# A hybrid decoder block on one core: the attention heads' last transposes and a LayerNorm's reductions go through DRAM instead of TensorE

## The chip, the cores and the metric

One core of a Trainium2 chip runs the whole kernel in one launch. The metric is the time of an execution on the device in microseconds; lower is better. The engines run side by side, each with its own in-order queue: TensorE (PE in the profile, its weight loads PEld), VectorE (DVE), ScalarE (ACT), GpSimd (POOL), and SyncE (SP), which issues nearly all DMAs.

## The reference

One layer over 512 tokens of width 2048, in float32:

```
h = RMSNorm(x);  proj = h @ W_in                       # 30 column tiles of 128
A: 8 heads x 64, dilated causal attention: the mixture of (window, dilation)
   (128,1), (512,4), (2048,16), combined by the softmax denominators
B: 512 channels: u * sigmoid(g) -> causal depthwise conv of 31 taps
   -> LayerNorm over channels -> silu
   mu = mean(y); var = mean((y - mu)^2); y = (y - mu) * rsqrt(var + EPS) * g + b
C: 16 query heads, 2 kv heads x 64, causal window of 128, with sinks
x = x + concat(A, B, C) @ W_out
x = x + (silu(RMSNorm(x) @ W_gate) * (RMSNorm(x) @ W_up)) @ W_down
```

In the A heads the weights exp(s) (queries in the partitions) have to be turned so that the keys stand in the partitions, to be multiplied by the values.

## The kernel before

Each float32 product is made of three matmuls on parts: a high part and a low part of both sides (`wh`, `wl` of the weights; `h_hi`, `h_lo` of the tokens), `wh*xh + wh*xl + wl*xh`, each 128x512. ScalarE casts the high parts (L295), VectorE subtracts to get the low ones (L269), two units of 128x1024 ahead of use, in three buffers each.

The stages are, in order: a head that projects the first four column tiles as the tokens come in; the other 26 projections of 16 x 3 matmuls (`project`), with the three mixers woven in; the output projection, in two halves of 16 tiles with 8 x 3 matmuls each (L1223 and on; the tiles' results are added to x by `residual`, L1166); the gated FFN by Strassen-like products (L1372 to L1375), and its down projection (L1637 to L1639).

What is woven in is set by hand. `Ticks` counts steps; a step passes after every two groups of three matmuls (in the output projection's second half after four). `ticks.after(n, fn)` puts `fn` n steps on, and at that step all engines' queues get the instructions that `fn` writes. So the place of everything relative to TensorE's queue is a number in the source, and a queue that is late keeps what stands behind it. The projections take the steps 0 to 207, the output projection begins at 208 (`T_MEET`), its second half at 272.

An A head (`attention("a", ...)`, one call for two heads) makes its scores in three units (`UNITS["a"]`): query blocks 0 and 1 together, block 2 (three key blocks), block 3 (four). For each: scores, scaling on ScalarE (L941), bias and minimum on VectorE (L946), exponentials on ScalarE (L954). Ten 128x128 blocks of weights result. Eight of them are turned through DRAM:

- `blocks_turn` (step t0+10): VectorE turns 32x32 squares into a 128x1024 tile `z` (L971).
- `blocks_leave` (two steps later): SP writes `z` to DRAM (`ed`, L976).
- `blocks_back` (three later): SP waits for that and reads it back by four strided DMAs into `et` (L983).
- `blocks_high`, `blocks_low` (five and six later): ScalarE's high copies `ph` (L993), VectorE's low parts `pl` (L999).

The other two blocks (key block 2 of query blocks 2 and 3) are turned by TensorE in `flip`: two transposes into a PSUM bank (L1006), with `high` (L1012) and `low` (L1017) behind. `weigh` multiplies all by the values (L1030, L1031). The heads come at least 8 steps apart; a0 and a1 lie in the projections, a2 and a3 in the output projection (t0 = 204, 212, 220 and 228).

In the same queues each q and k tile has a chain of its own for its RMS norm (`head_scales`): VectorE's turning sum, four small DMAs (L659), one back (L664), three POOL operations (L672 to L674); q's result scales the logits (L941).

The convolution is 124 operations of VectorE (`tap`, L590), spread over the steps by `TAP_TICKS`, with a pause round step 208. The LayerNorm behind it starts at `T_LN + 2`: `ln_sum` (L599 to L601), `ln_split` and `ln_center` (the mean through TensorE, `lnm`, L617 and L618), `ln_square`, then `ln_var`, where `transposed_scale` turns the squares' sum by four transposes (L486), reduces them on VectorE (L487) and takes the power on POOL (L489). `ln_out` spreads the scales to all partitions by four more transposes (L480) and multiplies (L633). `split_mix` makes the two parts of each row of the concatenation (L1085, L1086) for the output projection, which takes the `b` rows in its second half.

The RMS norm ahead already has another way for the same: `token_scale` and `spread`, with VectorE's turning sums and small DRAM trips.

Of the kernel before, what the change touches and what calls it, by code (L numbers as in the profile page):

```python
# [10 lines left out]
F32 = mybir.dt.float32  # L11
F32R = mybir.dt.float32r
# [3 lines left out]
ALU = mybir.AluOpType  # L16

P = 128
T = 512
NT = T // P  # L20
# [4 lines left out]
EPS = 1e-6  # L25
# [8 lines left out]
OUT_ORDER = (list(range(16)), [n + o for n in range(6) for o in (0, 8)] + [6, 7, 14, 15])  # L34

TAP_TICKS = (1.4, 1.5, 1.9, 1.9)
T_LN = 244
T_MEET = 208
T_GLU = 14

# [1 line left out]
SD, KD, VD, EV = 11, 6, 13, 1  # L42
# [79 lines left out]
def kernel(ctx: ExitStack, tc: tile.TileContext, xT, wi, wo, wgu, wd, cst_in, outT):  # L122
    nc = tc.nc
# [17 lines left out]
    ticks = Ticks()  # L141

    def slot(name, dt=F32, cols=T):
        return sp.tile([P, cols], dt, name=name, tag="s")

    def bank(name, cols=T, pool="banks"):
        return psum[pool].tile([P, cols], F32, name=name, tag="b")
# [64 lines left out]
    for t, (g, r) in enumerate(DOWN):  # L212
# [7 lines left out]
        for k in ("21A", "11A", "21B", "11B", "22A", "22B", "12A", "12B"):  # L220
            c = k[2]
# [130 lines left out]
    b = bank("idle")  # L352
# [4 lines left out]
    b = idle = None  # L357

    nhalf = cp.tile([P, 8], F32, name="nhalf")
# [3 lines left out]
    ident = cp.tile([P, P], F32, name="ident")  # L363
# [6 lines left out]
    def small(name, cols=NT):  # L370
        return cp.tile([P, cols], F32, name=name, tag="small", bufs=8)
# [56 lines left out]
    def token_scale(acc, n, name, after, then):  # L428

        part = cp.tile([P, NT, NT], F32, name=name + "p", tag="hsp", bufs=3)  # L430
        nc.vector.tensor_reduce(part.rearrange("p l b -> p b l"), acc.rearrange("p (b l c) -> p b l c", b=NT, l=NT),
                                axis=mybir.AxisListType.X, op=ALU.add, apply_transpose=True)

        def leave():
            d = tc.dram_tile([P, NT * NT], F32, name=name + "d")
            for a in range(4):
                nc.sync.dma_start(d.rearrange("(l i) (a b) -> i l a b", i=32, a=4)[:, :, a], part[32 * a:32 * a + 32])
            after(2, back, d)

        def back(d):  # L440
            t = cp.tile([P, 4, NT], F32, name=name + "t", tag="hst", bufs=3)
            nc.sync.dma_start(t.rearrange("p a b -> p (a b)"), d)
            after(3, power, t)

        def power(t):
            v = small(name + "v")
            wide = cp.tile([P, 64], F32, name=name + "w")
            r = wide[:, :NT]
            nc.gpsimd.memset(wide[:, NT:32], 0.0)
            nc.gpsimd.tensor_add(t[:, :2], t[:, :2], t[:, 2:])  # L450
            nc.gpsimd.tensor_add(v, t[:, 0], t[:, 1])
            nc.vector.tensor_scalar(v, v, 1.0 / n, EPS, op0=ALU.mult, op1=ALU.add)
            nc.gpsimd.tensor_tensor(r, v, nhalf[:, :NT], op=ALU.pow)
            then(v, r, wide)

        after(1, leave)
# [17 lines left out]

        ticks.after(2, turn)

    def spread_by_tensor(src4, name):
        b = bank(name)
        for i in range(NT):
            nc.tensor.transpose(b[:, i * P:(i + 1) * P], src4[:, i:i + 1].to_broadcast([P, P]), ident)  # L480
        return b

    def transposed_scale(acc, n, name):
        t, v, r = bank(name), small(name + "v"), small(name + "r")
        for i in range(NT):
            nc.tensor.transpose(t[:, i * P:(i + 1) * P], acc[:, i * P:(i + 1) * P], ident)  # L486
        nc.vector.tensor_reduce(v, t.rearrange("p (a b) -> p a b", b=P), axis=mybir.AxisListType.X, op=ALU.add)  # L487
        nc.vector.tensor_scalar(v, v, 1.0 / n, EPS, op0=ALU.mult, op1=ALU.add)
        nc.gpsimd.tensor_tensor(r, v, nhalf[:, :NT], op=ALU.pow)  # L489
        return r  # L490

    g4 = [bank(f"in{j}") for j in range(HEAD4)]
    h_hl = {}
    late_lows.append(True)
# [8 lines left out]
    for k in range(KT):  # L503
# [9 lines left out]
        elif k < 4 or k % 2 == 0:  # L513
            wh, wl = next_unit()
            o = 0
# [54 lines left out]
    hconv, yconv = {}, {}  # L570
# [24 lines left out]
    ln = {}  # L595
# [29 lines left out]
            add_square(ln["s"], yconv[j], j, "lq")  # L625

    def ln_var():
        ln["r"] = transposed_scale(ln.pop("s"), 512, "lv")

    def ln_out(mix):  # L630
        b = spread_by_tensor(ln["r"], "lrs")
        for j in range(NB):
            nc.vector.tensor_mul(yconv[j], yconv[j], b)  # L633
        for j in range(NB):
            nc.scalar.activation(yconv[j], yconv[j], AF.Silu, bias=col(C_LB + j), scale=col(C_LG + j))
            mix[f"b{j}"] = yconv[j]
# [179 lines left out]
    def attention(kind, box, mix, mi, heads):  # L816
        ready, every, step, s1, sx, s2, fl, ev, we = C_TICKS if kind == "c" else A_TICKS

        if mi in ROWS[-2:]:
            fl, we = fl + 2, we  # L820
        name = mi
# [29 lines left out]
        def head(h):  # L851
# [104 lines left out]

            ph, pl = {}, {}

            def block(i, j):
                for u, un in enumerate(us):  # L960
                    for ii, k0, n, o in un:
                        if ii == i:
                            f = o + j * P - k0
                            return es[u][:, f:f + P]

            def blocks_turn():
                z = wp.tile([P, 1024], F32, name=f"{name}z{h}", tag=f"raw{TURN_BUFS[0]}", bufs=1)
                to = z.rearrange("p (j b q) -> p b j q", j=4, b=8)
                for u, c, bs in ((0, slice(0, 2), slice(0, 2)), (0, slice(2, 3), slice(4, 5)), (1, slice(0, 2), slice(2, 6, 3)),
                                 (2, slice(0, 2), slice(3, 7, 3)), (2, slice(3, 4), slice(7, 8))):  # L970
                    nc.vector.transpose(to[:, bs], es[u].rearrange("p (b j q) -> p b j q", b=NT, j=4)[:, c])  # L971
                ticks.after(2, blocks_leave, z)

            def blocks_leave(z):
                d = tc.dram_tile([P, 1024], F32, name=f"{name}ed{h}")
                nc.sync.dma_start(d, z)  # L976
                ticks.after(3, blocks_back, d)

            def blocks_back(d):
                turned[0] = 3 - turned[0]  # L980
                t = wp.tile([P, 1024], F32, name=f"{name}et{h}", tag=f"raw{TURN_BUFS[turned[0]]}", bufs=1)
                for j in range(4):
                    nc.sync.dma_start(t[32 * j:32 * j + 32].rearrange("p (i c) -> p i c", i=4),  # L983
                                      d.rearrange("(i p) c -> p i c", i=4)[:, :, j * 2 * P:(j + 1) * 2 * P])
                ticks.after(5, blocks_high, t.rearrange("p (i b q) -> p b i q", i=4, b=8))

            def queries4(t):
                return t.rearrange("p (b i q) -> p b i q", b=NT, i=4)

            def blocks_high(src):  # L990
                for t in range(2):
                    ph[t] = slot(f"{name}ph{h}{t}", F32R)
                    nc.scalar.copy(queries4(ph[t]), src[:, NT * t:NT * t + NT])  # L993
                ticks.after(EV, blocks_low, src)

            def blocks_low(src):
                for t in range(2):
                    pl[t] = slot(f"{name}pl{h}{t}", F32R)
                    nc.vector.tensor_sub(queries4(pl[t]), src[:, NT * t:NT * t + NT], queries4(ph[t]).bitcast(F32))  # L999

            def flip(t):
                b = bank(f"{name}t{h}{t}")
                o = 0
                for j, i0, i1 in TBANKS[kind][t]:
                    for i in range(i0, i1 + 1):
                        nc.tensor.transpose(b[:, o:o + P], block(i, j), ident)  # L1006
                        o += P
                ticks.after(ev, high, t, b, o)

            def high(t, b, o):  # L1010
                ph[t] = slot(f"{name}ph{h}{t}", F32R)
                nc.scalar.copy(ph[t][:, :o], b[:, :o])  # L1012
                ticks.after(EV, low, t, b, o)

            def low(t, b, o):
                pl[t] = slot(f"{name}pl{h}{t}", F32R)
                nc.vector.tensor_sub(pl[t][:, :o], b[:, :o], ph[t][:, :o].bitcast(F32))  # L1017

            def weigh():
                b = bank(f"{name}o{h}")  # L1020
# [41 lines left out]
            if kind == "c":  # L1062
                ticks.after(tu, packed_exps)
                ticks.after(tu + s2, packed_norm)
                ticks.after(tu + 1, packed_turn)
            else:
                ticks.after(tu + s2, invert, h, den)
                ticks.after(tu + 2, blocks_turn)
                ticks.after(tu + s2 + fl + 2, flip, 2)
            ticks.after(t0 + at_v, weigh)  # L1070
            if h == 1:
                ticks.after(t0 + at_v - 2, sums_back)
# [21 lines left out]
    t_tap = T_GLU + 2  # L1094
    for j in range(NB):
        for i in range(TAPS):
            if T_MEET - 3 <= t_tap < T_MEET + 7:
                t_tap = T_MEET + 7
            ticks.after(int(t_tap), tap, j, i)
            t_tap += TAP_TICKS[j]  # L1100
    t_ln = T_LN
# [3 lines left out]
    ticks.after(t_ln + 4, ln_center)  # L1105
    ticks.after(t_ln + 6, ln_square)
    ticks.after(t_ln + 11, ln_var)
    ticks.after(t_ln + 14, ln_out, mix)
    for n, row in enumerate(r for r in ROWS if r[0] == "b"):
        ticks.after(t_ln + 15 + n, split_mix, row)  # L1110

    shared = {}
    cooling.append(True)
# [679 lines left out]
```

## Time and profile before

| | |
|---|---|
| Time, median of 3 runs | 1826.38 us (1826.2 to 1826.75) |
| Profiled execution | 1827.03 us, span 1825.3 us, clock 0.999 |
| TensorE busy | 1818.3 us, 8191 matmuls |
| VectorE, ScalarE, GpSimd busy | 1434.5, 1327.6, 1022.1 us |
| Output projection, first half | 375.5 to 474.4 us from the span's start |

A row of a timeline gives the start in us from the span's start, the length, the engine, the line and the operands (out<-in), the count of merged instructions, and in brackets the idle time before it and what ended that. Groups give the busy time, the mean length of one in ns, and the idle time ahead. Lists of waits give total, count and longest. Rows of stretches give for each engine the busy time and the count of instructions, then the granted clock, the DMA engines' busy share and GB/s. Matmuls overlap, so their lengths add up to more than the time that they take of the queue.

### The profile page before, as it was taken

What the parts mean: (1) busy time and instruction counts of PE and PEld (TensorE: products, weight loads), DVE (VectorE), ACT (ScalarE), POOL (GpSimd) and SP (SyncE); (2) the same over time, 40 slices, a digit from 0 to 9 for tenths busy, and PEclk for the clock granted to TensorE, in tenths of its full rate; (3) what the DMA queues carried; (4) which work ended last, traced back from release to release, by engine and by line L of the source; (5) the groups of instructions that cost most, each with busy time, mean ns of one, the idle gap of its engine ahead of it and who ended that gap; (6) DMA issues with size and microseconds to landing.
All of it is one profiled execution on the core that took longest, in us unless ns stands there. A gap on an engine that the chain in (4) does not pass through costs nothing.

```text
span 1825.3 us, 26570 instructions
## 1 busy us (share of the span) xinstructions
PE 1818.3 (100%) x8191; PEld 1509.9 (83%) x8191; DVE 1434.5 (79%) x1996; ACT 1327.6 (73%) x1848; POOL 1022.1 (56%) x793
## 2 busy tenths in 40 slices
PE   9999999999999999999999999999999999999998
PEld 7888888888888888888888888888888888888887
DVE  6779999987689777777777777777777777777777
ACT  6345656664468778888888888888887778877775
POOL 0116555120014577786887868878775568775652
PEclk9999999999999999999999999999999999999999
DMA  7355456666343557787777877778687579877645
GB/s 279 96 161 157 152 172 182 195 211 214 130 145 113 130 142 206 191 222 192 194 205 191 220 192 197 204 190 223 176 278 261 195 230 293 259 256 255 231 127 105
DMA packets 409295, 354.61 MB, mean 194 GB/s; under 512 B 177088, under 2 KB 331840, under 8 KB 409152
## 3 DMA queue, kind: packets, MB, share of 16 engines
q1 hardware_dynamic: 408576, 352.12, 65.7%
q8 instruction: 65, 1.06, 0.2%
q10 hardware_dynamic: 576, 0.79, 0.1%
q14 instruction: 78, 0.64, 0.1%
HBM read 270.00 MB, written 74.41 MB: 189 GB/s over the span
## 4 chain that ended last, share of the span: by engine, by line
PE 99%; DVE 1%; DMA 0%; issue 0%; ACT 0%; SPq 0%; DVEq 0%; ACTq 0%
PE out L1374 15%; PE out L1375 15%; PE out L1372 15%; PE out L1637 7%; PE out L1639 7%; PE out L1638 7%; PE o L328 3%; PE o L330 3%; PE o L329 3%; PE cq L328 2%; PE cq L329 2%; PE cq L330 2%; PE ak L328 1%; PE aq L328 1%; PE av L328 1%; PE ak L330 1%
## 5 line engine op out<-in xcount | busy, mean ns | idle before, releaser
L1372 PE MATMUL out<-wh,h 128*128 128x512 f32 x1232 | 479.2, 389 | 0.0
L1374 PE MATMUL out<-wl,h 128*128 128x512 f32 x1232 | 479.2, 389 | 0.0
L1375 PE MATMUL out<-wh,h 128*128 128x512 f32 x1232 | 479.2, 389 | 0.0
L1372 PEld LDWEIGHTS out<-wh,h 128*128 128x128 f32 x1232 | 231.2, 188 | 48.1
L1374 PEld LDWEIGHTS out<-wl,h 128*128 128x128 f32 x1232 | 231.2, 188 | 48.1
L1375 PEld LDWEIGHTS out<-wh,h 128*128 128x128 f32 x1232 | 231.2, 188 | 47.9
L1637 PE MATMUL out<-wh,a 128*128 128x512 f32 x620 | 240.4, 388 | 0.0
L1638 PE MATMUL out<-wl,a 128*128 128x512 f32 x620 | 240.3, 388 | 0.0
L1639 PE MATMUL out<-wh,a 128*128 128x512 f32 x620 | 240.3, 388 | 0.0
L295 ACT CAST wh<-w 128x1024 fp32r<-128x1024 f32 (+2 forms) x94 | 97.0, 1032 | 115.8 <-PE o L329 48.9
L1647 DVE TENSOR_TENSOR y<-y,out 128x512 f32<-128x512 f32 x192 | 128.6, 684 | 47.6 <-PE out L1639 46.1
L269 DVE TENSOR_TENSOR wl<-w,wh 128x1024 fp32r<-128x1024 f32 (+2 forms) x95 | 114.1, 1203 | 30.0 <-ACT wh L295 28.9
L1639 PEld LDWEIGHTS out<-wh,a 128*128 128x128 f32 x620 | 116.4, 188 | 24.0
L1638 PEld LDWEIGHTS out<-wl,a 128*128 128x128 f32 x620 | 116.4, 188 | 23.8
L1637 PEld LDWEIGHTS out<-wh,a 128*128 128x128 f32 x620 | 116.4, 188 | 23.8
L590 DVE SCALAR_TENSOR_TENSOR y<-bu,cst,y 128x511 f32<-128x511 f32 (+14 forms) x120 | 89.8, 748 | 0.5
L328 PE MATMUL o<-mh_c,wh 128*128 128x512 f32 x128 | 50.3, 393 | 0.0
L328 PE MATMUL cq<-hh,wh 128*128 128x512 f32 x128 | 50.0, 391 | 0.0
L329 PE MATMUL cq<-hl,wh 128*128 128x512 f32 x128 | 49.9, 390 | 0.0
L329 PE MATMUL o<-ml_c,wh 128*128 128x512 f32 x128 | 49.9, 390 | 0.0
L330 PE MATMUL o<-mh_c,wl 128*128 128x512 f32 x128 | 49.9, 390 | 0.0
L330 PE MATMUL cq<-hh,wl 128*128 128x512 f32 x128 | 49.8, 389 | 0.0
(2359 smaller groups left out, 4736.4 us busy)
## 6 DMA issues: line engine op xcount, KB each, us to landing
od<-a SPq DMA_DIRECT2D x154, 256.0 KB
a<-od SPq DMA_DIRECT2D x154, 256.0 KB
w<-in_wi SPq DMA_DIRECT2D x58, 512.0 KB
w<-in_wo SPq DMA_DIRECT2D x32, 512.0 KB
x<-in_xT SPq DMA_DIRECT2D x16, 256.0 KB
xr<-in_xT SPq DMA_DIRECT2D x16, 256.0 KB
x2d<-xr SPq DMA_DIRECT2D x16, 256.0 KB
z<-x2d SPq DMA_DIRECT2D x64, 64.0 KB
```

Of the source, the lines that this page charges most:

```text
L269: fn(*args)
L295: (nc.vector.tensor_copy if u == 0 else nc.scalar.copy)(hi[:, :n], t[:, :n])
L328: nc.tensor.matmul(out, wh, xh, start=start, stop=False)
L329: nc.tensor.matmul(out, wh, xl, start=False, stop=False)
L330: nc.tensor.matmul(out, wl, xh, start=False, stop=stop)
L1372: nc.tensor.matmul(b, x[:, high], wh[:, s], start=c == f == 0 and q in (7, 1, 5, 2), stop=False, skip_group_check=True)
L1374: nc.tensor.matmul(b, x[:, high], wl[:, s], start=False, stop=False, skip_group_check=True)
L1375: nc.tensor.matmul(b, x[:, low], wh[:, s], start=False, stop=c == f == 1, skip_group_check=True)
L1637: nc.tensor.matmul(b[:, lo:hi], x[:, high], wh[:, s], start=start, stop=False, skip_group_check=True)
L1638: nc.tensor.matmul(b[:, lo:hi], x[:, high], wl[:, s], start=False, stop=False, skip_group_check=True)
L1639: nc.tensor.matmul(b[:, lo:hi], x[:, low], wh[:, s], start=False, stop=last, skip_group_check=True)
L1647: getattr(eng, op)(t, t, src)
```

## The change

1. All ten blocks of an A head go through DRAM. `blocks_turn` makes a second tile `z2` (128x256) with two more turns, `blocks_leave` writes it, `blocks_back` reads it back by four DMAs into `t2`, and `blocks_high` and `blocks_low` make three copies and three subtractions instead of two. `block`, `flip`, `high`, `low` go. The exponentials' tiles are let go at `blocks_turn`.
2. The LayerNorm's variance takes `token_scale` and `spread` in place of the eight transposes; `spread_by_tensor` and `transposed_scale` go.
3. `T_LN` goes from 244 to 231, so `ln_sum` comes at step 233 instead of 246. From `ln_var` to `ln_out` there are 15 steps instead of 3, so `ln_out` comes at 259 instead of 260.
4. The pause of the taps ends at step 211 instead of 215.

```diff
-T_LN = 244
+T_LN = 231
...
     def ln_var():
-        ln["r"] = transposed_scale(ln.pop("s"), 512, "lv")
+        ln["r"] = slot("lrs")
+        token_scale(ln.pop("s"), 512, "lv", ticks.after, lambda v, r, wide: spread(wide, "l", ln["r"]))
 
     def ln_out(mix):
-        b = spread_by_tensor(ln["r"], "lrs")
         for j in range(NB):
-            nc.vector.tensor_mul(yconv[j], yconv[j], b)
+            nc.vector.tensor_mul(yconv[j], yconv[j], ln["r"])
...
                     nc.vector.transpose(to[:, bs], es[u].rearrange("p (b j q) -> p b j q", b=NT, j=4)[:, c])
-                ticks.after(2, blocks_leave, z)
+                z2 = slot(f"{name}z{h}", cols=2 * P)
+                to = z2.rearrange("p (j b q) -> p b j q", j=4, b=2)
+                for n in range(2):
+                    nc.vector.transpose(to[:, n], es[n + 1][:, 2 * P:3 * P].rearrange("p (j q) -> p j q", j=4))
+                es.clear()
+                ticks.after(2, blocks_leave, z, z2)
 
-            def blocks_leave(z):
+            def blocks_leave(z, z2):
                 d = tc.dram_tile([P, 1024], F32, name=f"{name}ed{h}")
                 nc.sync.dma_start(d, z)
-                ticks.after(3, blocks_back, d)
+                d2 = tc.dram_tile([P, 2 * P], F32, name=f"{name}ec{h}")
+                nc.sync.dma_start(d2, z2)
+                ticks.after(3, blocks_back, d, d2)
...
+                t2 = slot(f"{name}eu{h}", cols=2 * P)
+                for j in range(4):
+                    nc.sync.dma_start(t2[32 * j:32 * j + 32].rearrange("p (i c) -> p i c", i=4),
+                                      d2.rearrange("(i p) c -> p i c", i=4)[:, :, j * 64:(j + 1) * 64])
...
-            def flip(t):
-                b = bank(f"{name}t{h}{t}")
-                o = 0
-                for j, i0, i1 in TBANKS[kind][t]:
-                    for i in range(i0, i1 + 1):
-                        nc.tensor.transpose(b[:, o:o + P], block(i, j), ident)
-                        o += P
-                ticks.after(ev, high, t, b, o)
...
-                ticks.after(tu + s2 + fl + 2, flip, 2)
...
-            if T_MEET - 3 <= t_tap < T_MEET + 7:
-                t_tap = T_MEET + 7
+            if T_MEET - 3 <= t_tap < T_MEET + 3:
+                t_tap = T_MEET + 3
...
-    ticks.after(t_ln + 14, ln_out, mix)
+    ticks.after(t_ln + 26, ln_out, mix)
     for n, row in enumerate(r for r in ROWS if r[0] == "b"):
-        ticks.after(t_ln + 15 + n, split_mix, row)
+        ticks.after(t_ln + 27 + n, split_mix, row)
```

More of the change, by code (lines that the diff above doesn't have):

```diff
@@ L475, in spread @@
         ticks.after(2, turn)
[L477 to L490, printed above, removed]
     g4 = [bank(f"in{j}") for j in range(HEAD4)]
@@ L957, in head @@
             ph, pl = {}, {}
[L959 to L964, printed above, removed]
             def blocks_turn():
@@ L971, in blocks_turn, with blocks_back @@
                     nc.vector.transpose(to[:, bs], es[u].rearrange("p (b j q) -> p b j q", b=NT, j=4)[:, c])
-                ticks.after(2, blocks_leave, z)
-            def blocks_leave(z):
+                z2 = slot(f"{name}z{h}", cols=2 * P)
[5 more added lines that the diff above has]
+            def blocks_leave(z, z2):
                 d = tc.dram_tile([P, 1024], F32, name=f"{name}ed{h}")
                 nc.sync.dma_start(d, z)
-                ticks.after(3, blocks_back, d)
-            def blocks_back(d):
+                d2 = tc.dram_tile([P, 2 * P], F32, name=f"{name}ec{h}")
+                nc.sync.dma_start(d2, z2)
+                ticks.after(3, blocks_back, d, d2)
+            def blocks_back(d, d2):
                 turned[0] = 3 - turned[0]
@@ L984, in blocks_back @@
                                       d.rearrange("(i p) c -> p i c", i=4)[:, :, j * 2 * P:(j + 1) * 2 * P])
[L985 to L991, printed above, removed]
+                t2 = slot(f"{name}eu{h}", cols=2 * P)
+                for j in range(4):
+                    nc.sync.dma_start(t2[32 * j:32 * j + 32].rearrange("p (i c) -> p i c", i=4),
+                                      d2.rearrange("(i p) c -> p i c", i=4)[:, :, j * 64:(j + 1) * 64])
@@ L992, in blocks_high, with by_query @@
+                b8 = t.rearrange("p (i b q) -> p b i q", i=4, b=8)
+                ticks.after(5, blocks_high, (b8[:, :NT], b8[:, NT:], t2.rearrange("p (i b q) -> p b i q", i=4, b=2)))
+            def by_query(t, src):
+                return t[:, :src.shape[1] * P].rearrange("p (b i q) -> p b i q", i=4, q=32)
+            def blocks_high(srcs):
+                for t, src in enumerate(srcs):
                     ph[t] = slot(f"{name}ph{h}{t}", F32R)
-                    nc.scalar.copy(queries4(ph[t]), src[:, NT * t:NT * t + NT])
@@ L994, in blocks_high, with blocks_low @@
-                ticks.after(EV, blocks_low, src)
-            def blocks_low(src):
-                for t in range(2):
+                    nc.scalar.copy(by_query(ph[t], src), src)
+                ticks.after(EV, blocks_low, srcs)
+            def blocks_low(srcs):
+                for t, src in enumerate(srcs):
                     pl[t] = slot(f"{name}pl{h}{t}", F32R)
-                    nc.vector.tensor_sub(queries4(pl[t]), src[:, NT * t:NT * t + NT], queries4(ph[t]).bitcast(F32))
-            def flip(t):
-                b = bank(f"{name}t{h}{t}")
-                o = 0
-                for j, i0, i1 in TBANKS[kind][t]:
-                    for i in range(i0, i1 + 1):
-                        nc.tensor.transpose(b[:, o:o + P], block(i, j), ident)
-                        o += P
-                ticks.after(ev, high, t, b, o)
@@ L1010, in high @@
[L1010 to L1017, printed above, removed]
+                    nc.vector.tensor_sub(by_query(pl[t], src), src, by_query(ph[t], src).bitcast(F32))
             def weigh():
```

## The prediction

> **What bounds the kernel now.** I read the page first (its engines, its chain), then TensorE's own waits, then the groups of the instructions that the diff deletes, and last the timelines of the four other queues round the output projection's start, since that is where the change adds its work.
>
> ```profile
> span 1825.3 us, 26570 instructions
> ...
> PE 1818.3 (100%) x8191; PEld 1509.9 (83%) x8191; DVE 1434.5 (79%) x1996; ACT 1327.6 (73%) x1848; POOL 1022.1 (56%) x793
> ...
> PE 99%; DVE 1%; DMA 0%; issue 0%; ACT 0%; SPq 0%; DVEq 0%; ACTq 0%
> ```
>
> TensorE is the bound from end to end. Its whole list of waits has two lines, one ahead of the first warm-up matmul and one in the last output tile, both outside the stretch that is changed:
>
> ```profile
> PE idle L354 <- DVE nhalf L360: 1.1, 1, 1.1
> PE sides L1602 <- DVE y L1616: 1.1, 2, 0.6
> ```
>
> So in the mixers nothing ever makes TensorE wait. An instruction taken off its queue shortens the span by its share of the queue, and a wait put on it lengthens the span by its length; everything else is free until its cover is used up.
>
> **What leaves TensorE.** Eight heads lose two transposes each (16), the LayerNorm its four of the squares and four of the scales (24 in all):
>
> ```profile
> L1006 PE MATMUL a1t<-ident,a1e 128*128 128x128 f32 x4 | 0.8, 272 | 0.0
> ```
>
> The 272 ns are from start to end of one in a pipelined queue, so they are not what the queue pays. That is read from the starts of the neighbours. The undisturbed step is taken from the FFN, 1000.00 us over 4412 weight loads = 0.2267 us:
>
> ```profile
> 600.00:1600.00 1000.00, 1000.00 (x4413) 828.05 (x4412) 760.69 (x871) 820.60 (x993) 738.20 (x507) 1.00 0.74 209
> ```
>
> One pair of an A head, and the LayerNorm's first four (its other four have the same shape):
>
> ```profile
> 315.60 0.40 PE L330 MATMUL ak<-hh,wl 128*128 128x512 f32 x1
> 315.83 0.38 PE L1006 MATMUL a0t<-ident,a0e 128*128 128x128 f32 x2
> ...
> 317.21 0.39 PE L330 MATMUL ak<-hh,wl 128*128 128x512 f32 x1
> 454.43 0.39 PE L330 MATMUL o<-mh_c,wl 128*128 128x512 f32 x1
> 454.67 0.60 PE L486 MATMUL lv<-ident,lnv 128*128 128x128 f32 x4
> ...
> 456.96 0.40 PE L330 MATMUL o<-mh_c,wl 128*128 128x512 f32 x1
> ```
>
> From 315.60 to 317.21 lie six plain steps (two turns of the three lines): 1.61 - 6 x 0.2267 = 0.25 us for a pair, the few steps behind it that run at 0.23 to 0.24 included. From 454.43 to 456.96 lie nine: 2.53 - 9 x 0.2267 = 0.49 us for four. The gain is 8 x 0.25 + 2 x 0.49 = **2.98 us**, call it 3.0 (0.16%). The queue loses nothing else: the weighing matmuls keep their number and sizes.
>
> **What is put in its place, and on what.** ACT and VectorE keep the third copy and subtraction of each head at the same sizes; they only move from behind the flip to behind the other two. VectorE gains two 128x128 block turns per head: of the five existing turns' 1.45 us for 1024 columns (row `a2z` below), 256 more are 0.36 us, an estimate. In the LayerNorm one reduction is exchanged for another of the same 512 columns, and a small turn is added. None of it is on TensorE; the cover is the lead of the weights' low parts, which is smallest here (the third matmul of the output projection's third block needs the `wl` that VectorE ends at 386.34):
>
> ```profile
> 382.03 0.69 DVE L1086 TENSOR_TENSOR ml_a<-mix_a,mh_a 128x512 fp32r<-128x512 f32 x1 [2.29 <-ACT mh_a L1085]
> 385.12 1.22 DVE L269 TENSOR_TENSOR wl<-w,wh 128x1024 fp32r<-128x1024 f32 x1
> 386.94 1.45 DVE L971 STREAM_TRANSPOSE a2z<-a2e 128x256 f32<-128x256 f32 x5
> 388.16 0.19 PEld L330 LDWEIGHTS o<-mh_c,wl 128*128 128x128 f32 x1
> 389.02 0.73 DVE L590 SCALAR_TENSOR_TENSOR y<-bu,cst,y 128x490 f32<-128x490 f32 x1
> 389.66 1.22 DVE L269 TENSOR_TENSOR wl<-w,wh 128x1024 fp32r<-128x1024 f32 x1
> ```
>
> The lead is 388.16 - 386.34 = 1.8 us. The shorter pause of the taps sends the first tap at step 211 instead of 215, which is ahead of this `wl`: one tap, 389.66 - 389.02 = 0.64 us. That leaves 1.2 us. From the next block on two more taps than before stand ahead of each `wl`, until they run out at step 226 instead of 230.
>
> **SP's queue** gains five issues per head (one write, four reads): five at some 0.43 us, as in 1.75 us for four below, 2.2 us; and ten in the LayerNorm, some 4 us. Of what stands behind the first of them, one product is waited for:
>
> ```profile
> 358.16 2.02 SPq L983 DMA_DIRECT2D a1et<-a1ed  x4
> 360.60 2.50 SPq L659 DMA_DIRECT2D aq2d<-aq2p  x4
> 368.08 0.55 POOL L672 TENSOR_TENSOR aq2r<-aq2t 128x8 f32<-128x8 f32 x1 [19.09 <-DMA aq2t<-aq2d]
> 371.58 1.22 DVE L269 TENSOR_TENSOR wl<-w,wh 128x1024 fp32r<-128x1024 f32 x1
> 370.56 3.74 POOL L674 TENSOR_TENSOR aq2r<-aq2r,nhalf 128x8 f32<-128x8 f32 x1
> 374.33 0.82 ACT L941 ACTIVATE a2s<-a2s,aq2r 128x128 f32<-128x128 f32 x2 [4.06 <-POOL aq2r L674]
> 394.36 1.22 DVE L269 TENSOR_TENSOR wl<-w,wh 128x1024 fp32r<-128x1024 f32 x1
> 393.65 1.64 POOL L674 TENSOR_TENSOR aq3r<-aq3r,nhalf 128x8 f32<-128x8 f32 x1
> ```
>
> Behind this waiting ACT stand the casts that VectorE's 2.29 us wait is for, and behind that the `wl` with 1.2 us of lead. The new write and reads of head a1 stand ahead of `aq2d`, less the 0.42 us pause at 360.18: the chain begins up to 1.8 us later. POOL's power then takes 3.74 us again or 1.64 us as for aq3, so ACT's start moves by -0.3 to +1.8 us, and the stall is 0 to 0.6 us. I take 0.2: the slow power is the nearer row, but the 0.6 needs it at its full length, and SP without any pause behind 363.10.
>
> Why aq2's power is slow decides between the ends. It ran until 1.5 us after VectorE's last subtraction (371.58 + 1.22 = 372.80, idle then), as if it had begun only there. The Trainium skill, "SBUF — State Buffer", section "SBUF: two separate sides", says that a GpSimd operation and a VectorE operation with two SBUF inputs shut each other out for their whole length. By that rule a power that begins later meets an idle VectorE and ends where it ended before: no stall, and 1823.4 in place of the 1823.6 below. The row of aq3 speaks against it: its 1.64 us passed with VectorE's `wl` of 394.36 in the middle. I keep the bounds from the rows.
>
> **The round trip per head.** SP waits for the write to land before it reads back, with the next head behind it:
>
> ```profile
> 402.69 0.42 SPq L976 DMA_DIRECT2D a2ed<-a2z  x1
> 409.64 1.76 SPq L983 DMA_DIRECT2D a2et<-a2ed  x4
> ...
> 413.76 0.42 SPq L976 DMA_DIRECT2D a3ed<-a3z  x1
> ```
>
> A round, write to write, takes 413.76 - 402.69 = 11.1 us; the heads come every 8 steps, by two heads' weighings below 450.65 - 438.03 = 12.6 us. The round grows by 2.2 us of issue at most and by at least 256 KB of traffic:
>
> ```profile
> 392.00:394.00 2.00, 2.00 (x10) 1.68 (x9) 2.00 (x6) 1.39 (x4) 1.03 (x3) 1.00 0.93 144
> 402.00:404.00 2.00, 2.00 (x11) 1.65 (x10) 2.00 (x5) 1.98 (x6) 0.00 (x0) 1.00 1.02 341
> ```
>
> That is 256 KB at 341 GB/s, 0.8 us, up to 1.3 us with the reads at the 144 GB/s of a stretch of small packets. So 11.9 to 14.6 us if issue and traffic add up in full, against 12.6: level, or 2 us later per head. The third round ends 6 us late at worst; the last head's parts are ready at 442.14 and its weighing starts at 450.65, 8.5 us later, so nothing is felt:
>
> ```profile
> 440.86 1.28 DVE L999 TENSOR_TENSOR a3pl<-a3et,a3ph 128x512 fp32r<-128x512 f32 x2
> 438.03 0.39 PE L1030 MATMUL a3o<-a3ph,av 128*128 128x512 f32 x1
> 450.65 0.39 PE L1030 MATMUL a3o<-a3ph,av 128*128 128x512 f32 x1
> ```
>
> **The LayerNorm.** Sums, centring and squares move by 13 steps to about 414-430 us, beside heads a2 and a3.
>
> ```profile
> 413.70:430.60 16.90, 16.90 (x81) 14.12 (x81) 11.59 (x24) 9.13 (x20) 0.00 (x0) 1.00 0.77 240
> 423.67 1.21 DVE L269 TENSOR_TENSOR wl<-w,wh 128x1024 fp32r<-128x1024 f32 x1
> 432.57 0.19 PEld L330 LDWEIGHTS o<-mh_c,wl 128*128 128x128 f32 x1
> 439.65 0.69 DVE L610 TENSOR_TENSOR lnl<-lns,lnh 128x512 fp32r<-128x512 f32 x1 [2.77 <-ACT lnh L609]
> 443.40 0.39 PE L617 MATMUL lnm<-lnh,one 128*128 128x512 f32 x1
> ```
>
> VectorE is idle there for 16.90 - 11.59 = 5.3 us, and receives twelve operations of 512 columns at some 0.65 us, 7.8 us: leads shrink by 2.5 us, plus what its waits for ACT add. The low parts that end at 424.88 have 432.57 - 424.88 = 7.7 us; `lnl`, ended at 440.34, has 3.1 us. Cover enough, the second barely. The inverse root now comes through two DRAM trips and POOL: three steps (4 us) are given to the landing and two (2.7 us) to POOL's power of 1.64 to 3.74 us. Standing behind a late POOL in VectorE's queue are a residual's add, which frees a PSUM bank of the output projection, and the next `wl`. Stall: 0 to 1 us, taken as 0, by the quick power, since POOL does nothing else there (0.00 in the row). The scales are due one step sooner.
>
> The two or three slots more (the turned pair, its return, the scales) and the banks set free I cost at nothing: no wait of TensorE is for either.
>
> **The sum.** The profiled execution took 1827.03 us, 1.7 over its span and 0.65 over the runs' median. 1827.03 - 2.98 + 0.2 = 1824.25; against the median 1826.38, **1823.6 us**, 0.15% less. 0.2% is 3.65 us, about what the measurement can tell from no change, so the gain that I expect falls inside "the same".
>
> **The rivals.**
> - *The leads are used up* (23%): the `wl` at 386, `lnl` at its new place, a residual behind a VectorE that is kept by POOL. For it: leads of 1.8 and 3.1 us, and both SP and VectorE are full round 360 and 390. Against: each stall then lends its length to the next lead, so they do not add up. 0.5 to 3 us of the 3 return: 1824 to 1826.4.
> - *The round trip outgrows the heads' beat* (8%, slower): if the second write's landing is waited for in full after the first, one more 6.95 us (402.69 to 409.64) stands in each round, 11.1 + 2.2 + 6.95 = 20.2 against 12.6. Three rounds late by 7.6 each, less the 8.5 us of lead, stall 14 us: 1826.4 - 3.0 + 14 = 1837. It decides from a round of 12.6 + 8.5 / 3 = 15.4 us on, and the time is 1830.0 (slower) from 17.6 on. Against it: the second write is issued 0.4 us behind the first on the same queue, in a moment when DMA moves 341 GB/s.
> - *The transposes cost their length* (8%, faster): 24 x 0.272 = 6.5 us, 1819.9, if the queue behind pays the length and not the step; it decides from 3.65 / 24 = 0.152 us each on. Against it, starts 0.11 us apart (0.60 us for four, 272 ns the last). The Trainium skill, "TensorE: Matmul & The Clock Gate", Part 4: PE-mode transpose, gives some 275 ns for one in a kernel's context; the trace's 272 ns agree as a length, and by that figure the 24 would be 6.6 us.
> - *It does nothing* (3%): the FFN starts 3 us sooner and its DMA takes that back; 1826.4. Against: TensorE waits for no load there.
>
> **How the numbers follow.** The rest, 58%, is the forecast: no more than half a us lost, 1823.1 to 1824.0 with the runs' 0.3 us. The range for 8 in 10 adds the used-up leads: 1823.1 to 1826.5. Faster by over 0.2%: the transposes' 8%. Slower: the round trip's 8%. The same: 84%.
>
> **What would show it.** Right: TensorE's waits still have two lines; the third projection block's `wl` ends less than 1.8 us ahead; SP's rounds at 400-430 are 12 to 14.6 us long; no transposes but the last tile's. Wrong: a TensorE wait for `wl`, `xr`'s bank, `lnl` or `a3ph`, with its length; or a time below 1822.7.

## The result and the profile after

The changed kernel takes **1837.55 us** (median of 6 runs, 1834.0 to 1839.7) against 1826.5 us: ratio 1.006, 95% interval 1.0049 to 1.007. It is slower by 11 us (0.6%); forecast were 1823.6 us and a range up to 1826.5.

The page of the changed kernel, its span and its row of engines:

```profile
span 1838.0 us, 26617 instructions
...
PE 1818.9 (99%) x8167; PEld 1508.6 (82%) x8167; DVE 1438.0 (78%) x2013; ACT 1328.0 (72%) x1848; POOL 1025.8 (56%) x796
```

24 matmuls fewer, as meant (8191 to 8167), and TensorE's busy time is what it was: the 12.7 us more of span are not work. TensorE's waits in the changed kernel (in all, times, longest), where before had two lines:

```profile
PE o L328 <- DVE xr L1137: 7.8, 3, 4.4
PE a2s L848 <- DMA aq<-aq2l: 2.6, 1, 2.6
PE in L328 <- ACT wh L295: 1.6, 1, 1.6
PE idle L354 <- DVE nhalf L360: 1.1, 1, 1.1
PE sides L1573 <- DVE y L1587: 1.1, 2, 0.6
PE in L518 <- ACT hh L415: 0.2, 1, 0.2
```

Two new kinds in the changed stretch: the scores of head a2 wait for a small copy (`aq2l`), and tiles of the output projection wait for a bank that `residual` (`xr`) has not yet emptied. The 1.6 us for `wh` lie in the first 14 us, where nothing was changed; run again with a second profile (below, the change again) the kernel lacks them and keeps the rest:

```profile
PE o L328 <- DVE xr L1137: 9.1, 4, 5.0
PE a2s L848 <- DMA aq<-aq2l: 2.6, 1, 2.6
```

That second profile (span 1837.3 us) gives the clean account. The start of each matmul is compared with that of the same one before:

| Where | Shift of TensorE's queue, us |
|---|---|
| up to 317 us (nothing changed; scatter between executions) | -0.76 |
| a0's and a1's transposes | -1.07 |
| wait for `aq2l` at 370 us | +2.86 |
| residual of the output projection's third tile, 391 us | +2.75 |
| 391 to 451 us (a2's and a3's transposes, small shifts) | -0.20 |
| residual at 457 us (+1.55), and the LayerNorm's eight transposes (-0.97) | +0.59 |
| residual at 473 us | +5.19 |
| the matmuls behind it, at half rate | +2.72 |
| from there to the end | constant, +12.1 |

**First place.** SP's queue in the changed kernel's first profile, then before's second copy of `aq2l` and the first scores of a2:

```profile
365.39 2.15 SPq L968 DMA_DIRECT2D a1et<-a1ed  x4
367.65 1.79 SPq L972 DMA_DIRECT2D a1eu<-a1ec  x4
369.54 1.81 SPq L644 DMA_DIRECT2D aq2d<-aq2p  x4
371.96 0.59 SPq L688 DMA_DIRECT2D aq<-aq2l  x1
373.80 0.30 PE L848 MATMUL a2s<-ak2h,aq 128*128 128x128 f32 x1 [2.56 <-DMA aq<-aq2l]
```
```profile
363.71 0.59 SPq L703 DMA_DIRECT2D aq<-aq2l  x1
369.56 0.22 PE L863 MATMUL a2s<-ak2h,aq 128*128 128x128 f32 x1
```

Before, the copy was issued 5.85 us ahead of the scores. It now comes 8.25 us later, behind four added reads and a queue already late by a0's and a1's other added issues. The scores start when it has landed. POOL's power is late with it, and ScalarE's scaling and VectorE's part of the scores behind that (in the second profile 379.55 us against 376.32 before); two taps now come sooner as well, and the residual of the third tile stands behind all of it.

**Second place.** The LayerNorm's two trips in the changed kernel, on SP, VectorE and TensorE:

```profile
448.79 1.80 SPq L437 DMA_DIRECT2D lvd<-lvp  x4
453.98 0.34 SPq L442 DMA_DIRECT2D lvt<-lvd  x1
456.22 0.17 DVE L452 TENSOR_SCALAR lvv<-lvv 128x4 f32<-128x4 f32 x1 [4.83 <-POOL lvv L451]
462.91 0.34 SPq L472 DMA_DIRECT2D lrs<-le  x1
467.33 2.50 DVE L618 TENSOR_TENSOR y<-y,lrs 128x512 f32<-128x512 f32 x4 [3.40 <-DMA lrs<-le]
473.99 0.69 DVE L1137 TENSOR_TENSOR xr<-xr,o 128x512 f32<-128x512 f32 x1
474.83 0.54 PE L328 MATMUL o<-mh_c,wh 128*128 128x512 f32 x1 [4.40 <-DVE xr L1137]
475.17 0.63 PE L329 MATMUL o<-ml_c,wh 128*128 128x512 f32 x1
475.59 0.63 PE L330 MATMUL o<-mh_c,wl 128*128 128x512 f32 x1
```

From the first issue to VectorE's use of the scales it takes 18.5 us (19.2 us in the second profile). VectorE stands still twice with a residual behind it, and TensorE behind that. After the 4.40 us wait the matmuls start 0.42 to 0.43 us apart in place of 0.227, eight of them.

### The profile page after: what moved, and what is told of

The parts are those of the page before. It is cut to its first block, busy times and chain, and to the rows that moved or that the text cites. A ratio compares the mean times of both kernels' runs of the same rounds, so it can differ in the third digit from the quotient of the medians.

```text
span 1838.0 us, 26617 instructions
## 1 busy us (share of the span) xinstructions
PE 1818.9 (99%) x8167; PEld 1508.6 (82%) x8167; DVE 1438.0 (78%) x2013; ACT 1328.0 (72%) x1848; POOL 1025.8 (56%) x796
## 4 chain that ended last, share of the span: by engine, by line
PE 73%; DVE 1%; DMA 1%; ACT 0%; issue 0%; SPq 0%; DVEq 0%
PE out L1346 15%; PE out L1345 15%; PE out L1343 15%; PE out L1608 7%; PE out L1609 7%; PE out L1610 7%; PE o L328 2%; PE o L330 2%; PE o L329 2%; DMA out_T<-z 0%; DMA lrs<-le 0%; DVE y L1618 0%; DVE wl L291 0%; ACT y L620 0%; DMA le<-lvw 0%
```

## The experiments

Times of before, run beside them: 1826.4 to 1826.7 us. The expectations call the two heads of one call a pair.

**1. The heads alone.** LayerNorm and pause as before.

```
-T_LN = 231 ... ticks.after(t_ln + 26, ln_out, mix) ... T_MEET + 3
+T_LN = 244 ... ticks.after(t_ln + 14, ln_out, mix) ... T_MEET + 7   # and the transposes back in ln_var, ln_out
```

> The kernel before with the A heads' part of the change alone: LayerNorm, its place and the taps' pause as before. Theory A (SP's queue is full between 310 and 375 us, and five issues more in each of four heads add up to make aq2's copies late): the wait of a2's scores for aq<-aq2l stays (2 to 3 us), and the wait for a residual's bank at the third block of the output projection stays too (0 to 3 us); no wait behind 440 us. With 16 transposes less (2.0 us): 1826.5 - 2.0 + 2.6 + (0 to 2.6) = 1827 to 1830. Theory B (VectorE: taps and LayerNorm, moved sooner, use up its leads): no wait of a2's scores, 1824.5. If the first microseconds are slower again (2.6 us more than before), add 2.6 to either.

1829.84 us (10 runs), ratio 1.0019 (1.001 to 1.0029). Slower by 3 us, though 16 transposes are gone. TensorE waits 1.0 us for `aq2l`, 0.9 us at the third tile and 2.1 us at 451 us, the last with eight half-rate starts behind it (1.6 us):

```profile
453.61 0.49 PE L328 MATMUL o<-mh_c,wh 128*128 128x512 f32 x1 [2.07 <-DVE xr L1152]
443.42 1.14 ACT L998 CAST a3ph<-a3et 128x512 fp32r<-128x512 f32 x2 [3.24 <-DMA a3et<-a3ed]
444.07 1.29 DVE L1004 TENSOR_TENSOR a3pl<-a3et,a3ph 128x512 fp32r<-128x512 f32 x2 [2.08 <-ACT a3ph L998]
```

Theory A had no wait behind 440 us, so it holds for the first two waits alone. The last two rows tell why the third is there: ScalarE and VectorE stand still for a3's parts. These aren't needed for another 6 us, but in an in-order queue a residual stands behind them.

**2. The LayerNorm and the pause alone.**

```
(the change without the parts in blocks_turn ... blocks_low, flip, high, low)
```

> The kernel before with the LayerNorm's part alone: variance by turning sums and DRAM, thirteen steps sooner, the shorter pause of the taps; the A heads keep their flips. Theory D (the LayerNorm's own chain of two DRAM trips and POOL is too long for its 15 steps, and a residual stands behind it in VectorE's queue): the waits for xr at 450-475 us stay, 4 us and more with the slow steps behind a long wait: 1826.5 - 1.0 + 4 to 7 = 1829.5 to 1832.5. Rival (the chain is late only because SP stands behind head a3's eight reads): no wait there, 1825.5.

1832.3 us (6 runs), ratio 1.0031 (1.0019 to 1.0042). No wait for `aq2l`; VectorE waits for the scales, TensorE for the residual behind them:

```profile
460.00 2.50 DVE L618 TENSOR_TENSOR y<-y,lrs 128x512 f32<-128x512 f32 x4 [3.55 <-DMA lrs<-le]
PE o L328 <- DVE xr L1151: 4.2, 2, 4.0
```

So the trip is too long for its place even with no head's DMAs added. The parts alone shift TensorE's queue by 3.4 and 5.4 us, together 8.8 of the 12.1. Some 1.6 us of the rest arise already at `aq2l` (a wait of 2.6 us in the change, 1.0 us with the heads alone), at 370 us, ahead of all that the LayerNorm's part and the pause move; why is open.

**3. The change with a0 and a1 left as before.**

```
+if mi in ("a0", "a1"):  ... ticks.after(tu + s2 + fl + 2, flip, 2)   # their third group by TensorE again
```

> The changed kernel, but heads a0 and a1 keep their flips; a2 and a3 go through DRAM whole, LayerNorm as changed. Theory A: no wait of a2's scores for aq2l, none or a short one at the third block of the output projection; the LayerNorm's two waits (1.3 and 4.4 us, and 1.5 us of slow steps) stay. 1826.5 - 2.0 + 7.2 = 1831.7, or 1834.3 with a slow start. Theory B: the wait at the third block stays (2.6 us): 1834.3, or 1837 with a slow start.

1836.6 us (the median of three runs at clocks of 0.996 to 0.998), ratio 1.0051 (1.0035 to 1.0068); theory A's sum was 1831.7. The profiled execution has a mean clock of 0.461, but up to 1200 us its granted clock is 1.00 (0.97 from 400 to 500 us), so its mixers can be read:

```profile
PE o L328 <- DVE xr L1173: 7.2, 3, 5.7
```

The waits are those of theory A: none for `aq2l`, 0.5 us lost at the third tile, and residuals waited for 1.3 us at 452 and 5.7 us at 469 us. From 300 to 480 us TensorE's queue moves by 7.7 us (its shift goes from -0.9 to +6.8). The runs lost 10.2 us; where the rest goes is open, and so is how much a0 and a1 cost: 0.8 us by the runs (1837.5 against 1836.6), 5.3 by the two profiles (12.1 against 6.8).

**4. Five more issues per head, nothing else.** Before, with a write and four reads of a few bytes added.

```
+nc.sync.dma_start(tc.dram_tile([P, 1], F32, ...), nhalf[:, :1])
+for j in range(4): nc.sync.dma_start(cp.tile([P, 4], ...)[:32], cst_in[:32, :4])
```

> The kernel before with nothing of the change but five tiny DMAs more on SP's queue per A head, one write of 128x1 and four reads of 32x4 from a constant, at the places of the change's five; nobody waits for them and they move next to nothing. Theory A (issue time of SP's queue): a2's scores wait for aq2l nearly as in the changed kernel (1 to 3 us), and a wait at the third block follows (0 to 2.6): 1827.5 to 1832. Rival (it is the 256 KB more per head, or SP's waits for the second write's landing): no wait, 1826.5.

1872.59 us (1870.75 to 1873.62), 46 us above before; TensorE's and SP's waits:

```profile
PE a2s L863 <- DMA aq<-aq2l: 15.2, 1, 15.2
PE o L328 <- DVE xr L1169: 14.0, 4, 6.4
SPq L984 <- DMA a0ed<-a0z: 15.2, 2, 8.6
SPq L983 <- DMA a0ed<-a0z: 5.3, 2, 3.3
```

(the last row is before's.) The experiment failed as a measure of issue time: with a write of 128 rows of 4 bytes issued behind it, the big write `a0ed` was waited for 15.2 us in place of 5.3, and everything behind on SP with it. It shows only that transfers of such small rows are not free; whether the write or the four reads did it was not taken apart.

**5. LayerNorm alone, its end six steps later.**

```
-ticks.after(t_ln + 26, ln_out, mix)          +ticks.after(t_ln + 32, ln_out, mix)
-ticks.after(t_ln + 27 + n, split_mix, row)   +ticks.after(t_ln + 33 + n, split_mix, row)
```

> LayerNorm alone, as in the earlier run of that part, but with the scaling of y and the splits of its rows six steps later (6 x 0.68 = 4.1 us). Theory A, the trip through DRAM is longer than the fifteen steps that stand between the sums and the scaling, and VectorE holds a residual behind its wait for lrs (3.55 us in that run): the wait goes, TensorE's 4.0 us wait for xr and the 1.5 us of half-rate steps after it go with it, and what is left is the 0.6 us at the third block less the 0.98 us of the LayerNorm transposes: 1826 to 1827 us. Theory B, the rows of b are needed so soon that every later step is paid at their first use: TensorE waits for mh_b or ml_b, 1829 to 1833 us.

1826.59 us (10 runs), ratio 0.9999 (0.999 to 1.0009): 5.7 us back. A step is 1.36 us there (six matmuls), not the 0.68 that the expectation says; six are 8.2 us and more than is needed, the wait having been 3.55. Of TensorE's waits one is left beside the two of before, that of the third tile (experiment 7), and the scaling has no wait ahead:

```profile
PE o L328 <- ACT wh L295: 0.9, 1, 0.9
464.65 2.49 DVE L618 TENSOR_TENSOR y<-y,lrs 128x512 f32<-128x512 f32 x4
```

Theory A holds: what was short was the steps between the sums and the scales. The rows of `b` weren't needed sooner.

**6. The whole change with the same six steps.**

> The whole change with the same six steps more ahead of LayerNorm's scaling. Theory A: of the 5.8 us lost at the last residual wait (4.3 and 1.5) nearly all comes back if VectorE's 3.4 us wait for lrs was its cause: 1831 to 1833 us. With four heads' twins on SP's queue ahead of the small DMAs lrs may land later than these steps allow, then a wait of 1 to 2 us stays: 1833 to 1835 us. Theory B, the queue load alone sets it: 1836 to 1838 us as before.

1831.09 us (10 runs), ratio 1.0029 (1.0019 to 1.0038), 6.4 us less than the change. Left are 2.0 us for `aq2l`, 0.9 us at the third tile and 2.3 us for `xr` at 457 us, with half-rate starts behind the first and the last. The last isn't that of the heads alone: VectorE now stands still for the LayerNorm's first trip, whose write is issued behind a3's reads.

```profile
454.29 0.17 DVE L452 TENSOR_SCALAR lvv<-lvv 128x4 f32<-128x4 f32 x1 [5.12 <-POOL lvv L451]
```

**7. The pause alone.** Before with `T_MEET + 3` in place of `+ 7`.

> The kernel before with only the pause of the taps shortened from ten steps to six. By the lead of 1.8 us at the third output block, less one tap of 0.64 us, nothing is lost: 1826.4 us. By the shift of 0.64 us at that block which the run of LayerNorm alone showed, the pause loses it by itself: 1827.0 us. If the pause is what moves VectorE into the residual's way further on, a wait for xr over 1 us shows near 459 or 474 us: 1828 to 1831 us.

1827.38 us (10 runs), ratio 1.0003 (0.9994 to 1.0013): by the time no difference, by the profile a loss of 1.2 us at the third tile. VectorE and TensorE there, and the residual before:

```profile
387.23 0.72 DVE L590 SCALAR_TENSOR_TENSOR y<-bu,cst,y 128x489 f32<-128x489 f32 x1
387.87 0.68 DVE L1166 TENSOR_TENSOR xr<-xr,o 128x512 f32<-128x512 f32 x1
388.70 0.47 PE L328 MATMUL o<-mh_c,wh 128*128 128x512 f32 x1 [0.94 <-ACT wh L295]
386.25 0.68 DVE L1166 TENSOR_TENSOR xr<-xr,o 128x512 f32<-128x512 f32 x1
```

The residual ended at 386.93 before, 1.0 us ahead of the tile's first matmul at 387.93; two taps (0.64 us each) and a ScalarE copy ahead of them, 0.34 us late, put it 1.6 us later. The view names `wh` as releaser, but no `wh` ends there. What ends at 388.55 is `xr`, 0.15 us ahead of the matmul, as in the waits that the view puts down to `xr` (474.68 and 474.83 above), so I read the wait as the bank's.

**8. Which pairs?** Before, with the third group through DRAM in some pairs only (the others keep `flip`).

> The kernel before with the third group through DRAM in pairs a0 and a2 alone; a1 and a3 keep their flips, LayerNorm and the pause are as before. Theory A, the loss of the heads comes from two places only, the added issues of a1 ahead of aq2's row (TensorE's wait for a2s) and a3's trip in the LayerNorm stretch (the wait for xr at 451 us): neither is there, TensorE's waits stay the two lines of before, and eight transposes fewer give 4 x 0.25 = 1.0 us: 1825.4 us. Theory B, each pair's five issues cost their time on SP somewhere: 1827 to 1828 us, with a wait for aq2l or xr.

> The kernel before with the third group through DRAM in pair a3 alone. Theory A, a3's trip holds ScalarE's copies of a3ph and with them VectorE in the LayerNorm stretch, so that the residual near 451 us is late by about 2 us, and half-rate steps follow (1.5 us): 1826.5 - 0.5 + 3.5 = 1829.5 us, one wait for xr of about 2 us. Theory B, that wait needs the shift that a0 to a2 brought (their steps, banks and queue): no wait, 1826.0 us.

> The kernel before with the third group through DRAM in pairs a0, a2 and a3; a1 flips. Theory A, it is a1, by the a2s wait and the lateness of VectorE behind it, that made a3's trip late in the run of all heads: no wait for xr, 6 x 0.25 = 1.5 us fewer, 1825.0 us. Theory B, a2's added issues just ahead of a3 do that: a wait for xr of 1 to 2 us near 451 us, 1826 to 1828.5 us.

| Pairs | us (10 runs each) | ratio (95%) | TensorE's new waits | shift from transposes |
|---|---|---|---|---|
| a0, a2 | 1825.88 | 0.9996 (0.9987 to 1.0005) | 0.6 us for c6's scores, ahead of all that differs | -0.99 |
| a3 | 1826.12 | 0.9998 (0.9989 to 1.0007) | none | -0.51 |
| a0, a2, a3 | 1827.21 | 1.0004 (0.9995 to 1.0014) | 0.9 us at the third tile | -1.4, of it 1.1 lost |

a3 alone costs nothing, so the theory that its trip is late by itself fell. Nor is it late with a0 and a2 before it: in these profiles the wait at 451 us needs a1. The last line's time is 2 us over the 1825.0 of its theory A, and its 0.9 us are the bank again. TensorE comes 1.3 us sooner (a better start and the transposes) and the residual 0.6 us later than before, and the lead was 1.0. The residual's 0.6 us come from a2's chain on SP and POOL: ScalarE's scaling of its scores starts at 374.90 us against 374.33.

```profile
387.64 0.47 PE L328 MATMUL o<-mh_c,wh 128*128 128x512 f32 x1 [0.86 <-ACT wh L295]
```

**9. Place in the queue or traffic?** The change with the added DMAs on ScalarE's queue; and the change with only a1's last added reads one step later, behind aq2's DMAs on SP.

```
-nc.sync.dma_start(d2, z2)      +nc.scalar.dma_start(d2, z2)      # and the four reads alike
+if mi == "a1" and h == 1: ticks.after(1, back2, t2, d2)          # the other: a1eu's four reads
```

> The whole change, with the added write and the four added reads of each A head issued on ScalarE's queue in place of SP's; bytes and steps are the same. Theory A, it is the place on SP's queue ahead of aq2's small DMAs that makes aq2l late: TensorE's wait for a2s (2.6 us) goes or falls below 0.5 us, while the LayerNorm waits stay and ScalarE, which now stands still until each write has landed, may bring waits for wh of its own: 1832 to 1838 us. Theory B, it is the added traffic on the DMA engines: the wait for aq2l stays at 2 us or more. The time alone does not decide, the wait does.

> The whole change, but the four added reads of pair a1's second head (a1eu) are issued one step later, so that aq2's four small writes and two copies come ahead of them on SP's queue; the same bytes, the same count of issues. Theory A, aq2l is late by its place in that queue: its copies are issued 1.8 us sooner against the steps, and the wait for a2s falls from 2.6 to 0.8 us or less. Theory B, the traffic on the DMA engines makes it late: 2 us or more stays. The residuals' waits further on are there by both: 1833 to 1837 us.

On ScalarE's queue: 1838.5 us, ratio 1.007 (1.0054 to 1.0085), and the wait for `aq2l` is still 2.1 us. This didn't decide: ScalarE stood still for the added transfers, and VectorE 5.59 us behind it:

```profile
365.75 1.05 ACT L295 CAST wh<-w 128x1024 fp32r<-128x1024 f32 x1 [7.97 <-DMA a1eu<-a1ec]
```

The reads one step later: 1835.61 us (4 runs, 1832.86 to 1838.45), ratio 1.0049 (1.0035 to 1.0063). TensorE's waits:

```profile
PE o L328 <- DVE xr L1143: 6.3, 2, 5.0
PE a1o L1009 <- DVE a1pl L995: 2.5, 1, 2.5
PE a2s L848 <- DMA aq<-aq2l: 0.6, 1, 0.6
```

The same bytes and issues in another order, and the wait falls from 2.6 to 0.6 us (0.4 in experiment 11, which does the same): it is the place on SP's queue. But now a1's own parts come 2.5 us late. SP has no room there for both; one of the two consumers waits.

**10. The change again,** unaltered, for the slow start.

> The changed kernel once more, with a profile. Theory A, the 2.6 us lost in the first 14 us of the changed kernel's profiled execution (a late landing of x) belong to that execution and not to the change: the start is within 0.3 us of before's, the span about 1835.4 us, the time 1835 to 1838 us. Theory B, the change brings it: units start 2.6 us late from the first on again. The waits for a2s (2 to 3 us) and for xr near 395, 459 and 474 us (2.6, 1.3 and 4.4 us) are there by either.

1837.46 us, ratio 1.0061 (1.0048 to 1.0075), start 0.76 us sooner than before's. The slow start was that execution's.

**11. All pairs, every cause treated;** and the parts that gain alone.

```
all pairs: the change, a1's last reads one step later, t_ln + 32 and 33, T_MEET + 7
gains alone: pairs a0 and a2 alone, LayerNorm through DRAM with t_ln + 32 and 33, T_MEET + 7
```

> All that the change takes off TensorE, with each stall's cause taken away: a1's second reads behind aq2's copies, LayerNorm's scaling six steps later, the pause of the taps ten steps as before. Theory A, the stalls are SP's order, the steps given to LayerNorm's trip and the pause: the 3.0 us of transposes come out as forecast for the change, 1823.5 us, or up to 1825 us where a wait under 1 us for a2s is left. Theory B, four pairs of added issues also make a3's trip late in the LayerNorm stretch, as in the run of the heads alone: a wait for xr of about 2 us near 451 us with half-rate steps behind it, 1826 to 1828 us.

> A version meant to keep the gains alone: the third group through DRAM in pairs a0 and a2, LayerNorm's variance through DRAM with the scaling six steps later, the pause of the taps as before (ten steps). The parts measured so far: pairs a0 and a2 0.99 us off the later units, LayerNorm's sixteen transposes-worth 0.98 us, the pause's loss of 1.28 us not made. Theory A, these add up as nothing else touches them: 1826.5 - 1.0 - 1.0 = 1824.5 us, TensorE's waits those of before. Theory B, the long pause leaves the last taps too close to the sums, VectorE then keeps a residual: a wait for xr of 1 us or more, 1826 to 1828 us.

All pairs: 1829.67 us (11 runs), ratio 1.0016 (1.0007 to 1.0025), over the 1826 to 1828 of theory B, and by other waits than it named. a1's parts are late again, and VectorE holds a residual while it waits 5.0 us for `lvv`, whose trip starts behind a3's reads:

```profile
PE a1o L1009 <- DVE a1pl L995: 2.3, 1, 2.3
PE o L328 <- DVE xr L1143: 1.8, 1, 1.8
453.08 0.17 DVE L452 TENSOR_SCALAR lvv<-lvv 128x4 f32<-128x4 f32 x1 [5.00 <-POOL lvv L451]
```

The parts that gain: **1824.86 us** (11 runs, 1824.11 to 1826.38), ratio 0.9991 (0.9982 to 1.0), expected 1824.5. The fastest version here, 1.7 us under before, at the edge of what this can tell apart. Beside the two waits of before, TensorE has only 0.5 us at c6's scores:

```profile
PE c6s L848 <- DMA cq<-cq6l: 0.5, 1, 0.5
```

## Why the prediction was wrong

- **What leaves TensorE: right.** 0.25 us a head was forecast; a0's and a1's four heads gave 1.07 us, pair a3 0.51, pairs a0 and a2 0.99. A transpose costs its step, not its 272 ns.
- **SP's queue: the step that failed first.** It counted only a1's own added issues ahead of `aq2d` (up to 1.8 us) and followed only that one product. The second profile has

```profile
366.23 1.80 SPq L644 DMA_DIRECT2D aq2d<-aq2p  x4
```

  5.6 us later than before's 360.60, while TensorE's queue ran 1.07 us sooner by its transposes: the issues of all four heads of a0 and a1 add up, because SP has hardly a pause there (the second write of a1 already stands at 353.09 against 349.43). ScalarE's start, forecast to move by -0.3 to 1.8 us, moved by 3.2 from 374.33, though the power was the quick one, 1.64 us:

```profile
377.55 0.82 ACT L926 ACTIVATE a2s<-a2s,aq2r 128x128 f32<-128x128 f32 x2 [6.05 <-POOL aq2r L659]
```

  And the copies of `aq2l`, next on the same queue, have a consumer that I did not look up: a2's first scores, 5.85 us behind the issue. Priced 0.2 us; it cost 2.86.
- **The third tile: the wrong lead.** I took `wl`'s 1.8 us less one tap. Behind this `wl` stands the residual with 1.0 us, and the shorter pause puts two taps ahead of it. The pause alone lost 1.2 us; behind a late a2, 2.75.
- **The round trip: right in sum, not in each round.** Forecast were 11.9 to 14.6 us for every round, from one round of before. Write to write, the three rounds took 12.1, 10.8 and 17.8 us in the first profile of the change and 12.0, 12.6 and 17.0 in the second; before they were 11.4, 11.1 and 14.8, so the third was the long one already. Against TensorE's queue the last write came 5 to 6 us later, the 6 us that the prediction had at worst, and TensorE never waited for a3's parts. But "nothing is felt" was wrong: what waits is ScalarE and VectorE, and a residual stands behind them (experiment 1). A late operand costs by what is queued behind its reader, not by its own due time.
- **The LayerNorm: the term most mis-sized.** "Stall 0 to 1 us, taken as 0": it cost 5.19 + 2.72 us at its end. I gave each landing three steps, 4 us, from no row of this trip; the code gives each write two steps, 2.7 us, until its read is due. The two took 5.2 us (448.79 to 453.98) and 3.8 us (459.11 to 462.91) until the next issue, the last read 4.4 us more until VectorE began.
- **The rivals.** The mechanism was "the leads are used up", with its third place, a residual behind a VectorE kept by POOL, named; I had it at 23% and 0.5 to 3 us. Its ground "each stall lends its length to the next lead" failed: the second profile has waits of 2.6, 2.5, 1.3 and 5.0 us one after another. A late TensorE gave the residual of the third tile no lead, because VectorE was late by the same queue of SP, by way of POOL and ScalarE. The rival of the rounds did not come true: the third was longer than the beat of 12.6 us, but no read-back waited for a second landing in full (3.9 to 8.7 us from write to read, 5.0 to 7.1 before).
- **Not in any term:** half-rate matmuls behind a wait (below), 2.72 us.

Still open: whether all four pairs can gain. Experiment 11 leaves a1 without room on SP and `lvd` behind a3's reads; moving `lvd` ahead of these wasn't tried. So is why the two halves of the change cost more together than alone (experiment 2).

## What to carry to other kernels

Ahead of adding DMA issues to a queue that has no pauses, list everything behind them up to the next pause, and for each the consumer and its lead; issues accumulate over all the units that add them. When an in-order engine gets a new wait, the lead that counts is that of what stands behind the wait (here the residual that frees a bank, 1.0 us), not that of the awaited value. Give a trip through DRAM the length that a trip of the same kind shows in the trace (here 18.5 to 19.9 us from first issue to use), and take the place in the order from that. Price a wait of TensorE with the clock behind it: by the stretches below, one under 1.8 us costs its own length; one over 3.6 us (an estimate from two stretches of less than 1.8) comes with a fall of the clock, and such a fall cost 1.6 to 2.7 us more here; in between it depends on where the wait falls.

## What the runs showed of the hardware

A wait can cost more than its length. Behind some waits the granted clock falls to 0.50, and matmuls of 512 columns start 0.427 us apart in place of 0.227. Such a time lasts 3.41 us or a multiple of it, and within a trace these times begin whole multiples of 3.41 us apart (in experiment 6 at 372.00 and 457.33 us, 25 times 3.41). So each trace can be laid out in stretches of 3.41 us. Here are two of the heads alone, then two of the changed kernel with its 2.56 us wait for `aq2l`; the first figure behind the length is TensorE's busy time, the third from the end the granted clock:

```profile
451.32:454.73 3.41, 1.34 (x7) 0.96 (x7) 3.20 (x6) 0.58 (x1) 0.00 (x0) 1.00 0.71 239
454.73:458.14 3.41, 3.41 (x10) 2.56 (x9) 0.56 (x1) 0.00 (x0) 0.00 (x0) 0.50 0.87 285
369.27:372.69 3.42, 1.97 (x9) 1.31 (x7) 0.46 (x1) 2.46 (x6) 0.00 (x0) 1.00 0.25 39
372.69:376.10 3.41, 2.30 (x12) 2.03 (x13) 3.41 (x7) 2.01 (x4) 0.00 (x0) 1.00 0.95 247
```

In the first pair the whole wait of 2.07 us lies in one stretch, and the clock falls behind it; in the second the wait is divided, 1.44 and 1.11 us, and the clock stays. Over the profiles of all runs but experiment 3, from 20 to 1810 us, the clock fell behind each of the 15 stretches at full clock in which TensorE was idle for 1.79 us or more, and behind none with 1.75 us or less. It came back behind stretches with at most 0.33 us idle, and stayed down behind those with 0.48 us or more. So a wait of 2.0 us can be enough and one of 2.6 us need not be. The Trainium skill, "TensorE: Matmul & The Clock Gate", Part 1, has a window of about 3.4 us that runs freely, which agrees. It names an idle window as the condition, and here a window idle for little more than half of its length was enough.

Each added write took mostly 0.33 to 0.45 us of SP's queue, and four added reads mostly 1.8 us (2.0 to 2.4 in some places). On ScalarE's queue a1's four added reads held the engine for 7.97 us: some 5.3 us (357.77 to 363.04) until the first was issued, which I put down to the landing of the write that they read, and 2.67 us of issuing.

In five profiles a small POOL operation of aq2's chain ended 0.06 to 0.07 us behind VectorE's `wl`: in the pause alone at 372.63 us behind 372.57, after 5.42 us, in the second profile of the change at 375.53 behind 375.47, after 2.47. The same operation took 0.55 us before. That speaks for the exclusion which the prediction set aside by the row of aq3, but no run tests it.
